# A hybrid decoder layer: the gate products of the recurrence as pairs of 64-row matmuls

## The chip, the cores and the metric

The kernel runs on one core of one Trainium2 chip. The time is the device time of one execution in microseconds (us), lower is better. A run's profile is one profiled execution. PE is TensorE, PEld its weight loads, DVE VectorE, ACT ScalarE, POOL GpSimd, and SP the engine that issues most DMAs.

## What is computed

One layer of a decoder over 16 meta tokens and 1024 tokens of width 1024, in float32. Behind a combined input projection stand sliding-window attention (8 heads of 64) and a gated linear recurrence of width 512 side by side; then an output projection, a normalization, and a feed-forward layer of width 4096. What the change touches is the recurrence's gates:

```python
def rg_lru(x, w_a, b_a, w_x, b_x, lam):
    xb = x.reshape(bsz, t, LRU_BLOCKS, LRU_BLOCK)          # 8 blocks of 64
    gate_r = jnp.einsum("btnc,ncd->btnd", xb, w_a).reshape(bsz, t, LRU_WIDTH) + b_a
    gate_i = jnp.einsum("btnc,ncd->btnd", xb, w_x).reshape(bsz, t, LRU_WIDTH) + b_x
    r, i = jax.nn.sigmoid(gate_r), jax.nn.sigmoid(gate_i)
    log_a = -LRU_C * r * jax.nn.softplus(-lam)
    a, mult = jnp.exp(log_a), jnp.sqrt(-jnp.expm1(2.0 * log_a))
    u = mult * (i * x)
    # h[t] = a[t] * h[t-1] + u[t]
```

Each of the 8 blocks has its own 64x64 matrix for either gate: the product is block diagonal.

## The kernel before

Every matrix product is done in three passes: an operand is split into a rounded high part and a low remainder (`split`, lines 94 to 101: ScalarE's copy is line 96, VectorE's subtraction line 99), and `mm3` (lines 123 to 129) adds high by high (L125), high by low (L126) and low by high (L127). Tiles come from tags with a fixed number of buffers each (`bufs`, line 55: 8 of tag c, 17 of b, 4 of d, 2 of e, and two PSUM banks each of s, pt, o and acc); a tile waits until a buffer of its tag is free. Each engine executes its instructions in a fixed order. A scheduler sets that order from the order of the program and its own model of the times, and `behind` (line 106) and `lut` (line 81, all activation functions with tables) add further constraints of order.

The work is laid out with channels on partitions and tokens along the free dimension. The stages:

- input rows are normalized and transposed, keys, values, the first queries and the first chunk of x are projected (to about 55 us);
- eight half steps of attention, between which the projections of the other queries, of x and of y are filled in (`next_fill`, line 694; eight of ten fills lie here);
- the recurrence, from about 200 to 270 us: `gates`, then the last two fills (y of chunks 2 and 3, `fill_y`, line 671), then `decay` and `recur` by pairs of chunks, GeLU of y, `rec_out`, and in between the loads and splits of the output weights;
- the output projection, residual and normalization by rows (from about 235 to 300 us, its first part beside the recurrence), and the feed-forward layer to the end.

The recurrence works on 4 chunks of 128 channels, two blocks of 64 each, over 1040 tokens. The biases and other per-channel parameters are loaded as rows of `prm_r` (lines 355 to 358) and transposed on PE into `prm` (line 470).

The gates' weights: `graw` holds for either gate and each chunk a block diagonal 128x128 matrix. GpSimd sets it to zero (line 718), four DMAs put the 64x64 blocks on the diagonals (line 722), and `split` makes the high and low halves `gh` and `gl` (line 727).

`gates(c)` (lines 731 to 749) splits the chunk's x into `ch` and `cl`, and for each gate and each of three pieces of 348, 348 and 344 tokens takes the next PSUM bank, runs `mm3` on full 128 rows, and has ScalarE apply the sigmoid with that gate's bias into a tile of tag c. Then VectorE multiplies the input gate by x (line 749). These are 24 pieces, 72 products and 24 sigmoids.

`decay(c)` computes Exp and Tanh of the recurrence gate, `recur(c)` the square root on ScalarE and then on VectorE lines 762 and 763 and the scan (line 764); `rec_out` multiplies by the gelu of y (line 769) and splits the result, which the output projection reads.

Of the kernel before, what the change touches and what calls it, by code (L numbers as in the profile page):

```python
# [10 lines left out]
F32R = mybir.dt.float32r  # L11
AF = mybir.ActivationFunctionType
ALU = mybir.AluOpType
# [3 lines left out]
P = 128  # L17
D = 1024
KC = D // P
T = 1024  # L20
NMETA = 16
TT = T + NMETA
HD = 64
NPAIR = 4
NLRU = 4
# [12 lines left out]
def hybrid_layer(  # L38
# [6 lines left out]
    nc = tc.nc  # L45
# [12 lines left out]
    def slot(tag, shape, dt=F32):  # L58
        uid[0] += 1
        return slab.tile(shape, dt, tag=tag, name=f"{tag}{uid[0]}", bufs=bufs[tag])  # L60
# [4 lines left out]
    def bank(tag, shape=(P, 512)):  # L65
        uid[0] += 1
        return ps.tile(list(shape), F32, tag=tag, name=f"ps_{tag}{uid[0]}")

    def f32(ap):
        return ap.bitcast(F32)  # L70
# [8 lines left out]
    last_lut = [None]  # L79

    def lut(*args, **kwargs):
        ins = nc.scalar.activation(*args, **kwargs).ins  # L82
        if last_lut[0] is not None:
            tc.add_manual_dep(
                ins, last_lut[0],
                mybir.DependencyInfo(
                    mybir.DependencyClass.NoSync, mybir.DependencyReason.DATA
                ),
                reason="lut",
            )  # L90
        last_lut[0] = ins.name
        return ins

    def split(hi, lo, src, eng=None):
        if eng is None:
            nc.scalar.copy(hi, src)  # L96
        else:
            eng.tensor_copy(hi, src)
        low = nc.vector.tensor_tensor(lo, src, f32(hi), op=ALU.subtract).ins  # L99
        mark[0] = low.name  # L100
        return low
# [4 lines left out]
    def behind(name, *inss):  # L106
        for ins in inss:
            tc.add_manual_dep(
                ins, name,
                mybir.DependencyInfo(  # L110
                    mybir.DependencyClass.NoSync, mybir.DependencyReason.DATA
                ),
                reason="order",
            )
# [8 lines left out]
    def mm3(dst, lhs, rhs, start, stop):  # L123
        (lh, ll), (rh, rl) = lhs, rhs
        nc.tensor.matmul(dst, lh, rh, start=start, stop=False, skip_group_check=True)  # L125
        nc.tensor.matmul(dst, lh, rl, start=False, stop=False, skip_group_check=True)  # L126
        last_mm[0] = nc.tensor.matmul(  # L127
            dst, ll, rh, start=False, stop=stop, skip_group_check=True
        ).ins.name
# [45 lines left out]
    last_pow = [None]  # L175
# [90 lines left out]
    HALF = (slice(0, HD), slice(HD, P))  # L266
# [9 lines left out]
    flip = [0]  # L276
# [77 lines left out]
    nc.sync.dma_start(nsink, attn_sinks[0].partition_broadcast(P))  # L354
    prm_r = slot("d", [8, 512])
    nc.sync.dma_start(prm_r[0:4, :], conv_w[0])
    for i, src in enumerate((conv_b, b_a, b_x, lru_lambda)):
        nc.sync.dma_start(prm_r[4 + i : 5 + i, :], src)


    vk = [slot("b", [P, 8, P], F32R) for _ in range(2)]
# [68 lines left out]
    for b in range(4):  # L430
# [3 lines left out]
        if b == 0:  # L434

            acc = [bank("acc"), bank("acc")]
# [11 lines left out]
            for w, (t0, n), sink in ((wq, (16, 256), sink_q0), (wx, piece, sink_x0)):  # L448
                acc = bank("acc")
# [10 lines left out]
    for h in range(2):  # L460
        r, o, m = HALF[h], HALF[1 - h], slice(P - NMETA, P)
# [72 lines left out]
    def at_pair(cp):  # L534
        for half in range(2):
            at[half][cp] = pair("b", [P, 2, 512])


    def scores(j, half, q):

        sn = slot("c", [P, 2, 4, P + 1])
        negm = small.tile([P, 2, 4], F32, name="negm", tag="negm")
        den = small.tile([P, 2, 4], F32, name="den", tag="den")
        rden = small.tile([P, 2, 4], F32, name="rden", tag="rden")
        for h in range(2):
            nc.gpsimd.tensor_copy(
                sn[:, h, :, P], nsink[:, j + 4 * h : j + 4 * h + 1].to_broadcast([P, 4])
            )
        for h in range(2):
            for bp in range(2):  # L550
                sp_ = bank("s", (P, 2, 256))

                def qk(dst, b, hi, lo):
                    c = slice(b * P, (b + 1) * P)
                    nc.tensor.matmul(
                        dst, q[h][:, c], hi, start=True, stop=False,
                        skip_group_check=True,
                    )
                    nc.tensor.matmul(
                        dst, q[h][:, c], lo, start=False, stop=True,  # L560
                        skip_group_check=True,
                    )

                for i in range(2):
                    b = 4 * half + 2 * bp + i
                    if b == 0:
                        qk(sp_[:, i, 0:P], b, km[:, h, :], km[:, 2 + h, :])
                        qk(sp_[:, i, P:256], b, khh[h][:, 0:P], kl[h][:, 0:P])
                    else:
                        c = slice((b - 1) * P, (b + 1) * P)  # L570
                        qk(sp_[:, i, :], b, khh[h][:, c], kl[h][:, c])
                s_ = sn[:, h, 2 * bp : 2 * bp + 2, 0:P]
                nc.scalar.copy(s_, sp_[:, :, P:256])
                nc.vector.copy_predicated(
                    s_, above_i.rearrange("p (a b) -> p a b", a=1).to_broadcast([P, 2, P]),
                    sp_[:, :, 0:P],
                )
                if half == 0 and bp == 0:
                    w = slice(0, P - NMETA)
                    nc.vector.copy_predicated(sn[:, h, 0, w], above_i[:, w], far)  # L580
            nc.vector.tensor_reduce(
                negm[:, h, :], sn[:, h], axis=mybir.AxisListType.X, op=ALU.min
            )
            for k in range(4):
                lut(
                    sn[:, h, k, :], sn[:, h, k, :], AF.Exp, scale=-1.0,
                    bias=negm[:, h, k : k + 1], accum_out=den[:, h, k : k + 1],
                )
            nc.vector.reciprocal(rden[:, h, :], den[:, h, :])
            nc.vector.tensor_tensor(  # L590
                sn[:, h, :, 0:P], sn[:, h, :, 0:P],
                rden[:, h, :].to_broadcast([P, 4, P]), op=ALU.mult,
            )
        return sn
# [45 lines left out]
    xc = [None] * NLRU  # L640
# [11 lines left out]
            )  # L652
        xc[c] = y

    ys = [None] * NLRU

    def fill_q(j):
        def run(w):
# [11 lines left out]

    def fill_y(c):
        def run(w):
            y = slot("b" if c == 1 else "d", [P, T])

            def sink(acc, t0, n):
                nc.vector.tensor_copy(y[:, t0 - NMETA : t0 - NMETA + n], acc)

            project(w, REAL2, sink)
            ys[c] = y
        return run  # L680
# [13 lines left out]
    def next_fill():  # L694
        i = len(loaded) - 1
        if i + 1 < len(fills):
            loaded.append(fills[i + 1][0]())
        else:
            loaded.append(None)
        fills[i][1](loaded[i])  # L700

    prev = None
    for j in range(NPAIR):
        for half in range(2):
            if j % 2 == 0 and half == 0:
                at_pair(j // 2)
            sn = scores(j, half, qs[j])
            if True:
                with deferred(FILL_LAG):
                    next_fill()  # L710
            if prev is not None:
                attend(*prev)
            prev = (j, half, sn)
    attend(*prev)


    graw = slot("e", [P, 2, NLRU, P])
    behind(last_pow[0], nc.gpsimd.memset(graw, 0.0).ins)
    for i, w in enumerate((w_a, w_x)):
        for s in range(2):  # L720
            r = slice(HD * s, HD * s + HD)
            nc.sync.dma_start(
                graw[r, i, :, r], w[0, s::2].rearrange("n c d -> c n d")
            )
    gh = slot("e", [P, 2, NLRU, P], F32R)
    gl = slot("b", [P, 2, NLRU, P], F32R)
    split(gh, gl, graw)

    rg = [None] * NLRU

    def gates(c):
        ch, cl = pair("b", [P, TT])
        split(ch, cl, xc[c])
        rg[c] = []
        for i in range(2):
            t_ = slot("c", [P, TT])
            for t0, n in ((0, 348), (348, 348), (696, 344)):
                flip[0] += 1
                acc = bank(("s", "pt", "o")[flip[0] % 3])
                mm3(  # L740
                    acc[:, :n], (gh[:, i, c, :], gl[:, i, c, :]),
                    (ch[:, t0 : t0 + n], cl[:, t0 : t0 + n]), True, True,
                )
                lut(
                    t_[:, t0 : t0 + n], acc[:, :n], AF.Sigmoid,
                    bias=prm[:, c, 5 + i : 6 + i],
                )
            rg[c].append(t_)
        nc.vector.tensor_tensor(t_, t_, xc[c], op=ALU.mult)

    av = [None] * NLRU

# [37 lines left out]

    for c in range(NLRU):
        gates(c)
    for _ in range(2):
        next_fill()
    for cs in ((0, 1), (2, 3)):
        for c in cs:
            decay(c)
# [606 lines left out]
```

## Time and profile before

| | us |
|---|---|
| three runs: median (lowest to highest) | 965.29 (964.68 to 965.95) |
| the profiled execution | 966.98 |
| its span, first to last instruction | 965.3 |
| mean granted clock of PE | 0.998 |

The page of the profile lists each engine's busy time, a chain of the work that ended last, followed back from the end, and groups of instructions by line. L82 is `lut`, so all of the sigmoids, exponentials and roots have that line; L96 and L99 are `split`, and L125 to L127 `mm3`, whichever stage calls them. So one goes by stretches of time and by the names of tiles: `ps_s<-b,e` with 348 columns is a gate product, `ps_acc<-a,ws` a projection. In a row of the timeline stand start, duration, engine, line, operation, output and inputs with their shapes, a count, and in brackets the idle time before it with what ended it.

### The profile page before, as it was taken

To read this page: it belongs to the slowest core of one execution; us is meant where nothing else is said; L and a number is where in the kernel's file an instruction comes from. 1 tells how busy PE (TensorE), PEld (TensorE's weight loads), DVE (VectorE), ACT (ScalarE), POOL (GpSimd) and SP (SyncE) were. 2 spreads that over 40 slices of the span, in tenths; PEclk is the share of its full clock that TensorE was granted. 3 is DMA by queue.
4 is the path that set the end of the run, shared out by engine and by line. 5 is a ranking of instruction groups with operands and counts; after the bars stand their busy time and mean duration, and the time that the engine had idled before them with its cause. 6 is when DMAs were issued, how large, how long until landed. Compare 5 with 4: busy or idle time off the path is not lost.

```text
span 965.3 us, 12356 instructions
## 1 busy us (share of the span) xinstructions
PE 947.6 (98%) x4718; PEld 795.0 (82%) x4718; DVE 651.6 (68%) x833; ACT 503.2 (52%) x845; POOL 120.5 (12%) x183
## 2 busy tenths in 40 slices
PE   6999999999999999999999999999999999999996
PEld 6999999888878877888888888888888888888885
DVE  5567988856865695665654455468557676779884
ACT  6546765567744663443555566654433343436441
POOL 4202544500011100000000000000111100001201
PEclk9999999999999999999999999999999999999999
DMA  8121010013235457576423264324687765547934
GB/s 278 37 56 40 24 44 23 25 49 81 88 129 156 157 173 237 180 254 201 173 87 106 92 202 130 103 91 122 163 186 183 193 210 206 184 144 195 240 66 88
DMA packets 88155, 130.14 MB, mean 135 GB/s; under 512 B 13688, under 2 KB 52616, under 8 KB 88096
## 3 DMA queue, kind: packets, MB, share of 16 engines
q1 hardware_dynamic: 79504, 106.54, 34.0%
q0 software_dynamic: 8160, 21.51, 10.8%
q10 hardware_dynamic: 432, 1.31, 0.4%
q8 instruction: 37, 0.61, 0.3%
q14 instruction: 22, 0.18, 0.1%
HBM read 109.93 MB, written 18.87 MB: 133 GB/s over the span
## 4 chain that ended last, share of the span: by engine, by line
PE 81%; DVE 8%; ACT 4%; issue 3%; DMA 3%; POOL 1%; SPq 0%; DVEq 0%; ACTq 0%; POOLq 0%
PE ps_acc L125 9%; PE ps_acc L127 9%; PE ps_acc L126 9%; PE ps_pt L125 6%; PE ps_pt L127 5%; PE ps_pt L126 5%; PE ps_s L127 5%; PE ps_s L125 5%; PE ps_s L126 5%; PE ps_o L125 5%; PE ps_o L126 5%; PE ps_o L127 5%; ACT c L82 1%; PE ps_acc L253 1%; PE ps_o L620 1%
## 5 line engine op out<-in xcount | busy, mean ns | idle before, releaser
L96 ACT CAST ws<-raw 128x1024 fp32r<-128x1024 f32 (+1 forms) x68 | 69.6, 1024 | 120.7 <-PE ps_o L126 50.5
L99 DVE TENSOR_TENSOR ws<-raw,ws 128x1024 fp32r<-128x1024 f32 (+1 forms) x69 | 82.3, 1193 | 46.0 <-ACT ws L96 45.9
L125 PE MATMUL ps_acc<-a,ws 128*128 128x256 f32 (+2 forms) x256 | 85.8, 335 | 0.1
L126 PE MATMUL ps_acc<-a,ws 128*128 128x256 f32 (+2 forms) x256 | 85.4, 334 | 0.0
L127 PE MATMUL ps_acc<-a,ws 128*128 128x256 f32 (+2 forms) x256 | 84.9, 332 | 0.0
L99 DVE TENSOR_TENSOR b<-b,b 128x1024 fp32r<-128x1024 f32 (+2 forms) x48 | 57.5, 1199 | 32.3 <-PE ps_o L126 19.4
L96 ACT CAST ws<-e 128x1024 fp32r<-128x1024 f32 x41 | 42.9, 1045 | 65.4 <-PE ps_o L126 45.9
L96 ACT CAST b<-b 128x1024 fp32r<-128x1024 f32 (+2 forms) x47 | 48.8, 1037 | 37.3 <-DVE b L905 37.3
L99 DVE TENSOR_TENSOR ws<-e,ws 128x1024 fp32r<-128x1024 f32 x41 | 50.1, 1222 | 19.6 <-ACT ws L96 19.6
L609 POOL TENSOR_SCALAR_AFFINE_SELECT c<-c 128x512 fp32r<-128x512 f32 x64 | 52.6, 837 | 71.8 <-ACT c L96 61.9
L125 PEld LDWEIGHTS ps_acc<-a,ws 128*128 128x128 f32 x256 | 48.2, 188 | 4.6 <-ACT c L396 0.4
L127 PEld LDWEIGHTS ps_acc<-a,ws 128*128 128x128 f32 x256 | 48.2, 188 | 4.3
L126 PEld LDWEIGHTS ps_acc<-a,ws 128*128 128x128 f32 x256 | 48.2, 188 | 4.0
L125 PE MATMUL ps_acc<-ws,b 128*128 128x512 f32 (+1 forms) x120 | 46.2, 386 | 0.0
L127 PE MATMUL ps_acc<-ws,b 128*128 128x512 f32 (+1 forms) x120 | 46.2, 385 | 0.0
L126 PE MATMUL ps_acc<-ws,b 128*128 128x512 f32 (+1 forms) x120 | 46.1, 384 | 0.0
L125 PE MATMUL ps_pt<-ws,b 128*128 128x512 f32 x112 | 44.3, 395 | 0.0
L126 PE MATMUL ps_pt<-ws,b 128*128 128x512 f32 x112 | 44.1, 394 | 0.0
L127 PE MATMUL ps_pt<-ws,b 128*128 128x512 f32 x112 | 44.0, 393 | 0.0
L125 PE MATMUL ps_s<-ws,b 128*128 128x512 f32 x110 | 43.5, 395 | 0.0
L127 PE MATMUL ps_s<-ws,b 128*128 128x512 f32 x110 | 43.4, 394 | 0.0
L126 PE MATMUL ps_s<-ws,b 128*128 128x512 f32 x110 | 43.3, 394 | 0.0
(394 smaller groups left out, 2658.9 us busy)
## 6 DMA issues: line engine op xcount, KB each, us to landing
raw<-in_w_ff_dram SPq DMA_DIRECT2D x61, 512.0 KB, 3.8
e<-in_w_ff_dram SPq DMA_DIRECT2D x45, 512.0 KB, 3.8
d<-in_w_ff_dram SPq DMA_DIRECT2D x12, 512.0 KB, 3.8
s_dram<-d POOLq DMA_DIRECT2D x12, 512.0 KB, 4.0
raw<-in_w_in_dram SPq DMA_DIRECT2D x9, 512.0 KB, 4.6
c<-in_x_dram SPq DMA_DIRECT2D x8, 512.0 KB, 9.1
d<-in_x_dram SPq DMA_DIRECT2D x8, 512.0 KB, 4.8
out_dram<-raw SPq DMA_DIRECT2D x8, 512.0 KB, 2.6
```

Source lines behind the costliest of these rows:

```text
L82: ins = nc.scalar.activation(*args, **kwargs).ins
L96: nc.scalar.copy(hi, src)
L99: low = nc.vector.tensor_tensor(lo, src, f32(hi), op=ALU.subtract).ins
L125: nc.tensor.matmul(dst, lh, rh, start=start, stop=False, skip_group_check=True)
L126: nc.tensor.matmul(dst, lh, rl, start=False, stop=False, skip_group_check=True)
L127: last_mm[0] = nc.tensor.matmul(dst, ll, rh, start=False, stop=stop, skip_group_check=True).ins.name
L253: last_mm[0] = nc.tensor.matmul(acc[:, :n], w[k // 2][:, kc, :], u[kc][k % 2][:, t0 : t0 + n], start=k == 0 and kc == 0, stop=k == last an ...
L609: nc.gpsimd.affine_select(out=p_[:, :, s], in_=f32(p_[:, :, 0]), pattern=[[0, 4], [g, P]], compare_op=op, fill=0.0, base=0, channel_multip ...
L620: nc.tensor.matmul(po[:, oc : oc + n], v, p_[:, pc : pc + n], start=first and k == 0, stop=last and k == 1, skip_group_check=True,)
```

## The change

The weights of either gate no longer form block diagonal matrices. `graw` becomes [128, 4, 128]: partitions 0 to 63 hold a chunk's first block and partitions 64 to 127 its second; along the columns stand the two gates of that block, the recurrence gate first in the first block, and the input gate first in the second. Nothing need be set to zero. High and low halves share a tile `gw`.

`gates(c)` now takes two PSUM banks for each piece of tokens. For each of the three passes it issues two products one after the other, on rows 0 to 63 and on rows 64 to 127, each with 128 columns of weights, and each into its own bank. Their results hold both gates of one block, so the sigmoid's outputs `z[0]` and `z[1]` hold both gates mixed. The biases are laid out to match (four DMAs in place of two).

A new function `gather(c)` puts them apart: VectorE copies the input gate of the first block and of the second into a tile `gi`, 64 partitions each, GpSimd copies the recurrence gate of the second block into `z[0]`, and VectorE multiplies `gi` by x. For chunks 0 and 1 it is called behind their gates; for chunks 2 and 3 behind the fill of y's chunk 2, and placed behind that fill's first copy on VectorE. y of chunk 2 and `gi` of chunks 2 and 3 take buffers of tag b. The rounding of the weights (`gw[:, 0]`) is placed behind the last table function that precedes the last half step of attention.

```diff
--- before.py
+++ after.py
@@ -354,8 +354,15 @@
     nc.sync.dma_start(nsink, attn_sinks[0].partition_broadcast(P))
     prm_r = slot("d", [8, 512])
     nc.sync.dma_start(prm_r[0:4, :], conv_w[0])
-    for i, src in enumerate((conv_b, b_a, b_x, lru_lambda)):
-        nc.sync.dma_start(prm_r[4 + i : 5 + i, :], src)
+    for i, src in ((4, conv_b), (7, lru_lambda)):
+        nc.sync.dma_start(prm_r[i : i + 1, :], src)
+
+    for i, src in enumerate((b_a, b_x)):
+        for s in range(2):
+            nc.sync.dma_start(
+                prm_r[5 + s : 6 + s, :].rearrange("o (c t k) -> t o c k", t=2, k=HD)[i ^ s],
+                src.rearrange("o (c t k) -> t o c k", t=2, k=HD)[s],
+            )
 
 
     vk = [slot("b", [P, 8, P], F32R) for _ in range(2)]
@@ -652,7 +659,7 @@
             )
         xc[c] = y
 
-    ys = [None] * NLRU
+    ys, y_copies = [None] * NLRU, {}
 
     def fill_q(j):
         def run(w):
@@ -670,10 +677,11 @@
 
     def fill_y(c):
         def run(w):
-            y = slot("b" if c == 1 else "d", [P, T])
+            y = slot("b" if c in (1, 2) else "d", [P, T])
 
             def sink(acc, t0, n):
-                nc.vector.tensor_copy(y[:, t0 - NMETA : t0 - NMETA + n], acc)
+                ins = nc.vector.tensor_copy(y[:, t0 - NMETA : t0 - NMETA + n], acc).ins
+                y_copies.setdefault(c, ins.name)
 
             project(w, REAL2, sink)
             ys[c] = y
@@ -704,6 +712,7 @@
         for half in range(2):
             if j % 2 == 0 and half == 0:
                 at_pair(j // 2)
+            gate_after = last_lut[0]
             sn = scores(j, half, qs[j])
             if True:
                 with deferred(FILL_LAG):
@@ -714,39 +723,53 @@
     attend(*prev)
 
 
-    graw = slot("e", [P, 2, NLRU, P])
-    behind(last_pow[0], nc.gpsimd.memset(graw, 0.0).ins)
+
+    graw = slot("e", [P, NLRU, P])
     for i, w in enumerate((w_a, w_x)):
         for s in range(2):
-            r = slice(HD * s, HD * s + HD)
             nc.sync.dma_start(
-                graw[r, i, :, r], w[0, s::2].rearrange("n c d -> c n d")
-            )
-    gh = slot("e", [P, 2, NLRU, P], F32R)
-    gl = slot("b", [P, 2, NLRU, P], F32R)
-    split(gh, gl, graw)
+                graw[HALF[s], :, HALF[i ^ s]],
+                w[0, s::2].rearrange("n c d -> c n d"),
+            )
+    gw = slot("e", [P, 2, NLRU, P], F32R)
+    behind(gate_after, nc.scalar.copy(gw[:, 0], graw).ins)
+    nc.vector.tensor_tensor(gw[:, 1], graw, f32(gw[:, 0]), op=ALU.subtract)
 
     rg = [None] * NLRU
 
     def gates(c):
         ch, cl = pair("b", [P, TT])
         split(ch, cl, xc[c])
-        rg[c] = []
-        for i in range(2):
-            t_ = slot("c", [P, TT])
-            for t0, n in ((0, 348), (348, 348), (696, 344)):
+
+
+        z = [slot("c", [P, TT]) for _ in range(2)]
+        for t0, n in ((0, 348), (348, 348), (696, 344)):
+            acc = []
+            for s in range(2):
                 flip[0] += 1
-                acc = bank(("s", "pt", "o")[flip[0] % 3])
-                mm3(
-                    acc[:, :n], (gh[:, i, c, :], gl[:, i, c, :]),
-                    (ch[:, t0 : t0 + n], cl[:, t0 : t0 + n]), True, True,
+                acc.append(bank(("s", "pt", "o")[flip[0] % 3]))
+            for k, (a, b) in enumerate(((0, ch), (0, cl), (1, ch))):
+                for s in range(2):
+                    nc.tensor.matmul(
+                        acc[s][:, :n], gw[HALF[s], a, c, :], b[HALF[s], t0 : t0 + n],
+                        start=k == 0, stop=k == 2, skip_group_check=True,
+                    )
+            for s in range(2):
+                lut(
+                    z[s][:, t0 : t0 + n], acc[s][:, :n], AF.Sigmoid,
+                    bias=prm[:, c, 5 + s : 6 + s],
                 )
-                lut(
-                    t_[:, t0 : t0 + n], acc[:, :n], AF.Sigmoid,
-                    bias=prm[:, c, 5 + i : 6 + i],
-                )
-            rg[c].append(t_)
-        nc.vector.tensor_tensor(t_, t_, xc[c], op=ALU.mult)
+        rg[c] = z
+
+
+    def gather(c):
+        z, gi = rg[c], slot("b" if c > 1 else "c", [P, TT])
+        first = nc.vector.tensor_copy(gi[HALF[0]], z[0][HALF[1]]).ins
+        nc.gpsimd.tensor_copy(z[0][HALF[1]], z[1][HALF[1]])
+        nc.vector.tensor_copy(gi[HALF[1]], z[1][HALF[0]])
+        nc.vector.tensor_tensor(gi, gi, xc[c], op=ALU.mult)
+        rg[c] = z[0], gi
+        return first
 
     av = [None] * NLRU
 
@@ -790,8 +813,12 @@
 
     for c in range(NLRU):
         gates(c)
-    for _ in range(2):
-        next_fill()
+        if c < 2:
+            gather(c)
+    next_fill()
+    for c in (2, 3):
+        behind(y_copies[2], gather(c))
+    next_fill()
     for cs in ((0, 1), (2, 3)):
         for c in cs:
             decay(c)
```

## The prediction, made before the change was run

> **What bounds the kernel now.** I read the page's busy line first, then the busy time by stretch around the gates, then the chain of waits there.
>
> ```profile
> PE 947.6 (98%) x4718; PEld 795.0 (82%) x4718; DVE 651.6 (68%) x833; ACT 503.2 (52%) x845; POOL 120.5 (12%) x183
> ```
> ```profile
> 203.50:221.20 17.70, 17.70 (x98) 16.27 (x98) 7.23 (x8) 13.84 (x27) 0.00 (x0) 1.00 0.12 31
> 221.20:229.50 8.30, 8.30 (x38) 6.77 (x37) 3.65 (x5) 8.19 (x8) 0.00 (x0) 1.00 0.25 62
> 229.50:269.36 39.86, 39.65 (x172) 31.82 (x171) 36.37 (x37) 27.02 (x33) 0.00 (x0) 1.00 0.28 88
> ```
> The columns are the stretch and its length in us, then busy time and count of PE, PEld, DVE, ACT and POOL, then the granted clock (1.00 throughout) and the DMA share. The gates lie in the first stretch. PE is busy all of it. VectorE works 7.23 of 17.70 us there, and 36.37 of 39.86 us in the third stretch, where the recurrence is computed. GpSimd does nothing in all three.
>
> The chain of waits runs, from the sigmoids on, not over PE but over ScalarE and VectorE:
>
> ```profile
> 218.71 0.96 ACT c L82 x2
> ...
> 221.17 1.28 ACT L82
> ...
> 228.39 1.08 ACT c L82
> 229.50 2.40 DVE c L762 x2
> ...
> 268.05 0.61 DVE d L769
> 268.69 0.63 ACT b L96
> 269.36 0.50 PE ps_pt L125
> ```
> Sigmoid, table load, Exp and Tanh, Sqrt, the recurrence, the product with the gelu, its rounding, and then the output projection on PE. PE has other work meanwhile (projections and output products of other chunks), and that work is used up just as the chain arrives:
>
> ```profile
> 269.36 0.50 PE L125 MATMUL ps_pt<-a,b 128*128 128x512 f32 x1 [0.21 <-ACT b L96]
> ```
> PE waits 0.21 us there. So between 201.6 and 269.36 there are **two bounds of almost one length**: PE's own work, and the chain that begins with the first sigmoid. The kernel gains the smaller of what the two gain. Behind 269.36 I see no stage held to a clock time of its own, so I let a gain there run through to the end.
>
> **PE's work.** Now there are 24 pieces of three products, 72 in all. First and last of one unbroken run of 21:
>
> ```profile
> 212.63 0.32 PE L125 MATMUL ps_s<-b,e 128*128 128x348 f32 x1
> ...
> 215.79 0.32 PE L127 MATMUL ps_s<-b,b 128*128 128x348 f32 x1
> ```
> 20 steps in 3.16 us are 0.158 us a step (the 0.32 us is one product's passage, half of it under the next). 72 x 0.158 = 11.4 us. Afterwards there are again 72 products, of the same columns but 64 rows each, in 36 pairs whose two members use different rows of the array and different PSUM banks. Call the step of a pair p. No row of this trace shows two products side by side, so p is bounded: below by 0.158, one product's step, if the members overlap wholly; above, as long as their weights still load ahead, by 0.316, two steps. For the weights I look at the only products on few rows that are followed by their like, the parameter transposes:
>
> ```profile
> 55.08 0.38 PE L306 MATMUL ps_o<-ident,d 128*128 128x128 f32 x2
> 55.29 0.38 PE L306 MATMUL ps_s<-ident,d 128*128 128x128 f32 x2
> 55.60 0.41 PE L469 MATMUL ps_o<-ident,d 8*128 8x8 f32 x4
> 55.95 0.44 PE L528 MATMUL ps_pt<-ident,c 128*128 128x128 f32 x2
> ```
> ```profile
> L469 PE MATMUL ps_o<-ident,d x4: 202/202/223, 55.6 to 55.8; 8*128 8x8 f32 x4
> ```
> Four of them, each with a weight load of 128 columns, take 0.41 us from first start to last end, and one takes 0.20 us, so they start 0.07 us apart. Two loads a pair, 0.14 us, fit under 0.158. I take p = 0.18, near the lower end, with 0.02 for the second member: 36 x 0.18 = 6.5 us, **4.9 us less**.
>
> By the Trainium skill (TensorE: Matmul & The Clock Gate, Part 3: packing small matmuls), products on different row groups start within about 4 ns of each other, and four row tiles gave 3.07 times the speed, 77% of four. At 77% of two, as an estimate from that page, p would be 0.206, and PE would save 4.0 us.
>
> What speaks against the change is in the same rows. The first 8-row load is not issued under the running transpose:
>
> ```profile
> 55.60 0.26 PEld L469 LDWEIGHTS ps_o<-ident,d 8*128 8x128 f32 x3 [0.17 <-issue]
> ```
> PEld stands 0.17 us idle although nothing is waited for. The full-row transposes step by 0.105 us (55.08 and 55.29 each head two); the next product begins about 0.2 us behind the last one, and on the way back 0.14 us behind. So **a change of rows costs about 0.1 us** (0.05 to 0.15). The Trainium skill (TensorEngine Tiling (Array Packing), Key Properties) has the rule: changing the tiling mode drains the array. The trace agrees, with this 0.17 us.
>
> How many changes? Between the gate products PE now runs projection products of full rows; their counts in five gaps:
>
> ```profile
> 202.52:202.98 0.46, 0.45 (x2) 1.00 0.00 0
> ...
> 204.91:208.13 3.22, 3.22 (x14) 1.00 0.00 0
> ...
> 210.53:210.75 0.22, 0.21 (x1) 1.00 0.00 0
> ...
> 211.24:212.62 1.38, 1.38 (x6) 1.00 0.00 0
> ...
> 215.95:218.02 2.07, 2.07 (x9) 1.00 0.79 202
> ```
> Five gaps make six stretches of gates, 12 changes, 1.2 us (0.6 to 1.8). PE in all: 36p + 1.2 - 11.4, which at p = 0.18 is **-3.7 us** (-5.1 to +1.8 from the bounds).
>
> **The chain's work.** Its first part is ScalarE's:
>
> ```profile
> 204.85 0.55 ACT L82 ACTIVATE c<-ps_s,prm 128x348 f32<-128x348 f32 x1
> ...
> 207.03 1.08 ACT L96 CAST b<-b 128x1040 fp32r<-128x1040 f32 x1
> ...
> 213.37 0.55 ACT L82 ACTIVATE c<-ps_s,prm 128x348 f32<-128x348 f32 x1 [1.38 <-PE ps_s L127]
> 213.81 0.55 ACT L82 ACTIVATE c<-ps_pt,prm 128x348 f32<-128x348 f32 x1
> ...
> 218.71 0.55 ACT L82 ACTIVATE c<-ps_pt,prm 128x348 f32<-128x348 f32 x1 [1.95 <-PE ps_pt L127]
> ...
> 220.60 0.55 ACT L82 ACTIVATE c<-ps_o,prm 128x344 f32<-128x344 f32 x1
> ```
> From 204.85 to 221.15 are 16.3 us. Sigmoids that wait for nothing step by 0.44 us: 24 x 0.44 = 10.6, and one rounding of 1.0 is between them, 11.6. The remaining 4.7 us are waits for PE (1.38 and 1.95 the longest). With the products ready 3.7 us or more sooner, up to **4.7 us** of this goes. ScalarE's count and shapes stay.
>
> Then VectorE, which gets 8 copies of 64x1040 (two a chunk), and GpSimd, which gets 4. The nearest rows:
>
> ```profile
> L98 DVE CAST ws<-raw x1: 694/694/694, 223.8 to 223.8; 128x1024 fp32r<-128x1024 f32 x1
> ```
> ```profile
> L644 DVE TENSOR_SCALAR d<-d,prm x2: 809/812/816, 102.8 to 140.7; 128x1040 f32<-128x1040 f32 x2
> ...
> L644 DVE TENSOR_SCALAR b<-d,prm x1: 1130/1130/1130, 178.6 to 178.6; 128x1040 f32<-128x1040 f32 x1
> ```
> ```profile
> 157.51 0.63 POOL L609 TENSOR_SCALAR_AFFINE_SELECT c<-c 128x512 fp32r<-128x512 f32 x1 [3.99 <-ACT c L96]
> ...
> 177.49 4.76 POOL L609 TENSOR_SCALAR_AFFINE_SELECT c<-c 128x512 fp32r<-128x512 f32 x4 [0.24 <-DVE c L99]
> ```
> A copy between SBUF tiles of 1024 columns took 0.69 us; the same tensor_scalar took 0.81 alone and 1.13 while GpSimd was at work beside it. I take 0.70 a copy, 5.6 us in all (up to 1.13, 9.0 us). GpSimd at 0.63 us for 512 columns alone and 1.2 beside VectorE needs 1.3 to 2.4 us a copy. Two places matter:
> - The gathers of chunks 0 and 1 fall in the first stretch, where VectorE has over 10 us free; the projections run on PE meanwhile. If that cover were gone, they would cost their 2.8 us.
> - The gathers of chunks 2 and 3 wait for y's copy and stand on VectorE's queue **ahead of the recurrence** (L762), with two copies and the product with x (now L749) each: 2 x (1.4 + 1.24) = 5.3 us. L762 could then start 4.7 us sooner, near 224.8, and between the last sigmoid (216.5) and there 8.3 us are free less two splits and copies of y (about 3 us now). They fit with nothing over; I charge 1.7 us of collision (0 to 4).
>
> ```profile
> L749 DVE TENSOR_TENSOR c<-c,d x3: 1234/1241/1242, 209.3 to 216.3; 128x1040 f32<-128x1040 f32 x3
> ```
> So the chain gains 4.7 - 1.7 = **3.0 us** (-0.5 to 5). Exp and Tanh of a chunk also wait for GpSimd's copy into z[0]: its 1.3 to 2.4 us lie under the later chunks' sigmoids for chunks 0 to 2, and chunk 3 is needed only at the second Exp round, 20 us later. The third chunk's tiles in tag c take the buffers that the first gathers free; that wait is in the 1.7.
>
> **Edits at nothing.** The memset goes from GpSimd, idle around it. The weights' split halves (VectorE's is 1.2 us before 198, under projections on PE); its rounding moves to behind the last softmax but one, long before use. Two DMA issues of biases are added on SP:
>
> ```profile
> 18.73 0.22 SPq L358 DMA_DIRECT2D d<-in_b_x_dram  x1
> 20.01 0.22 SPq L358 DMA_DIRECT2D d<-in_lru_lambda_dram  x1
> 21.34 2.21 SPq L198 DMA_DIRECT2D raw<-in_w_in_dram  x3
> ```
> They step by 1.3 us, so the weight load behind them starts up to 2.6 us later, and what they load is used first at 55.60; PE's work on other projections covers that. Without the cover it would be the 2.6 us.
>
> **The sum.** PE -3.7, chain -3.0; the smaller gain decides: -3.0 us. The profiled execution, 966.98 us with a span of 965.3, would become 964.0; against the median of the runs shown, 965.29, that is **962.3 us**.
>
> **Rivals.**
> - *The pairs do not run side by side* (the change doesn't do what it says). Then 36p grows: PE changes by 36p - 10.2. At p = 0.316 it is +1.2; and if each load waits for the product before it, as at the change of rows, about 0.25 us a product, p = 0.5 and +7.8. It turns slower by 0.2% from p = 0.34. For it: no overlap is seen in this trace, and the load at 55.60 did wait. Against: that wait shows at changes only; 8-row loads then follow each 0.07 us. Time 966.5 to 973, likeliest about 968.
> - *VectorE becomes the bound.* Sigmoids come sooner, but the late gathers (5.3 to 7.4 us) go into the third stretch, which has 3.5 us free; the chain ends where it ended or a little later, and PE stands idle instead. For it: 91% busy there. Against: 10 us free before. Time 964.5 to 966.5.
> - *Evacuation sets the pace.* By the Trainium skill (TensorEngine Tiling, PSUM Bottleneck), tiling speeds TensorE but not the emptying of PSUM. Here ScalarE's 11.6 us of the 16.3 are that limit, and the chain's 4.7 us already stop at it. If all else goes well, PE saves 5.1 and the chain 4.7: 960.6.
>
> **How the numbers follow.** Forecast, with its own range 960.6 to 963.3 us: 0.50. All goes well, 959.2 to 960.6: 0.12. VectorE the bound: 0.16. Pairs in sequence: 0.22, of which 0.02 near 966.5. A measurement of this kernel can tell 0.2%, 1.9 us, from no change. Faster 0.50 + 0.12 = 0.62; within 0.2%, 0.16 + 0.02 = 0.18; slower 0.20. The range leaves out the slowest sequences and the luckiest orders of instructions: 959.2 to 968.
>
> **What would show it.** In the profile after: pairs at L125's successor starting a few ns apart, with steps near 0.18 us; a gap of about 0.1 us at each change of rows; the sigmoids within 12 to 13 us; L762's first start near 226; PE's wait at the output projection's last chunk 0.5 to 1.5 us, filled by VectorE, not PE. Pair steps over 0.3 us, or L762 not earlier, would make it wrong, and so would a wait that grows behind 269 us.

## The result, and the profile after

| | before | after |
|---|---|---|
| median of six runs (lowest to highest), us | 965.71 (964.68 to 966.87) | 961.86 (960.82 to 963.93) |
| ratio, 95% interval | | 0.9962 (0.9951 to 0.9973) |
| profiled execution, its span, us | 966.98, 965.3 | 963.93, 962.1 |
| first gate product to first transpose behind the output projection, us | 201.59 to 291.21: 89.62 | 202.01 to 287.40: 85.39 |

The change took 3.85 us off; 962.3 us was forecast, 3.0 less than the 965.29 known then. The last row measures the stage by itself in the profiled executions, free of what varies ahead of it (in the thirteen profiles the first gate product lay between 199.96 and 202.99 us, whatever the kernel): 4.23 us less. It compares the same work: in it PE's timeline lists 335 products of 512 columns before and 336 after, besides the 72 of the gates. Later, between 340 and 380 us, where PE waits for the next stage's first operands, its waits grew from 1.43 to 1.79 us, so a little (0.36 us) is given back.

The busy line of the page after:

```profile
PE 943.7 (98%) x4718; PEld 789.4 (82%) x4718; DVE 658.9 (68%) x841; ACT 502.0 (52%) x845; POOL 125.0 (13%) x186
```
PE has the same 4718 products and 3.9 us less of busy time; VectorE has the eight copies and 7.3 us more. The gate products of the first chunk in PE's timeline after, from the last projection product ahead of them to the second behind:

```profile
201.69 0.40 PE L125 MATMUL ps_acc<-a,ws 128*128 128x512 f32 x1
202.01 0.43 PE L753 MATMUL ps_s<-b,e 64*128 64x348 f32 x1
202.02 0.42 PE L753 MATMUL ps_pt<-b,e 64*128 64x348 f32 x1
202.28 0.32 PE L753 MATMUL ps_s<-b,e 64*128 64x348 f32 x1
202.28 0.31 PE L753 MATMUL ps_o<-b,e 64*128 64x348 f32 x1
202.43 0.32 PE L753 MATMUL ps_pt<-b,e 64*128 64x344 f32 x1
202.44 0.32 PE L753 MATMUL ps_o<-b,e 64*128 64x344 f32 x1
...
203.38 0.32 PE L753 MATMUL ps_pt<-b,e 64*128 64x344 f32 x1
203.38 0.32 PE L753 MATMUL ps_o<-b,e 64*128 64x344 f32 x1
203.63 0.50 PE L126 MATMUL ps_acc<-a,ws 128*128 128x512 f32 x1
203.96 0.39 PE L127 MATMUL ps_acc<-a,ws 128*128 128x512 f32 x1
```
Two products start within 0.01 us of each other, and each is as long as a full-row one (0.32 us). From the second pair to the ninth the step is (203.38 - 202.28) / 7 = **0.157 us a pair**, where one full-row product took 0.158. The price stands at the ends: 0.32 us from the projection to the first pair (its own step is 0.23), 0.27 to the second, 0.25 from the last pair to the projection (a pair's step is 0.157), 0.33 to the next. Over the usual steps that is 0.09 + 0.11 us on the way in and 0.09 + 0.10 on the way out, so by these rows each change of rows costs about **0.2 us**. PEld's timeline shows the same hole at the change:

```profile
202.01 0.18 PEld L753 LDWEIGHTS ps_s<-b,e 64*128 64x128 f32 x1 [0.36 <-issue]
...
203.62 0.19 PEld L126 LDWEIGHTS ps_acc<-a,ws 128*128 128x128 f32 x1 [0.22 <-issue]
```
Each chunk's pairs stand in one stretch (starts 202.01, 207.30, 211.22 and 215.12), so there are 8 changes. ScalarE's sigmoids, first and last, and what it waited for:

```profile
204.44 0.55 ACT L82 ACTIVATE c<-ps_s,prm 128x348 f32<-128x348 f32 x1
...
208.13 0.55 ACT L82 ACTIVATE c<-ps_s,prm 128x348 f32<-128x348 f32 x1 [0.94 <-PE ps_pt L753]
...
212.06 0.55 ACT L82 ACTIVATE c<-ps_s,prm 128x348 f32<-128x348 f32 x1 [1.17 <-PE ps_pt L753]
...
215.96 0.55 ACT L82 ACTIVATE c<-ps_s,prm 128x348 f32<-128x348 f32 x1 [1.14 <-issue]
...
218.14 0.58 ACT L82 ACTIVATE c<-ps_o,prm 128x344 f32<-128x344 f32 x1
```
They take 14.3 us in place of 16.3. ScalarE still waits ahead of each chunk but the first (the profile names PE for two of the three waits), because PE's order puts projection products between the chunks' pairs. VectorE's timeline, the gather of chunk 2 and the start of the two recurrences:

```profile
215.75 0.70 DVE L767 COPY b<-c 64x1040 f32<-64x1040 f32 x1
216.49 0.69 DVE L769 COPY b<-c 64x1040 f32<-64x1040 f32 x1
217.21 1.98 DVE L770 TENSOR_TENSOR b<-b,d 128x1040 f32<-128x1040 f32 x1
...
227.14 2.39 DVE L785 SCALAR_TENSOR_TENSOR c<-b,c 128x1040 f32<-128x1040 f32 x2 [2.15 <-ACT c L82]
...
255.36 4.53 DVE L787 TENSOR_TENSOR_SCAN c<-b,b 128x1040 f32<-128x1040 f32 x2
```
The recurrence (L785) begins 2.36 us sooner by the clock of the trace, 2.8 us measured from the first gate product. It waited for ScalarE, not for the gathers ahead of it. The last two scans stand back to back from 255.36. Before, the last one began at 263.34:

```profile
256.50 2.31 DVE L764 TENSOR_TENSOR_SCAN c<-b,c 128x1040 f32<-128x1040 f32 x1
...
263.34 2.31 DVE L764 TENSOR_TENSOR_SCAN c<-b,c 128x1040 f32<-128x1040 f32 x1
```
In VectorE's timeline before, three splits of the output weights (253.06, 259.87 and 262.21, 1.2 us each) and a product with the gelu (261.00, two in 1.28) stand among the last two chunks' recurrences. After, all seven splits of these weights are done by 248.8, and the products stand behind the scans.

At the output projection PE waits for nothing any more:

```profile
262.00:266.80 4.80, 4.80 (x22) 3.91 (x21) 3.90 (x7) 1.74 (x4) 0.00 (x0) 1.00 0.31 109
266.80:290.00 23.20, 23.20 (x106) 18.96 (x106) 13.66 (x21) 11.60 (x31) 5.40 (x10) 1.00 0.26 98
```
So the chain that the prediction had as the nearer bound no longer holds PE up here. What follows tests this, and whether the overlap is really the source.

### The profile page after: what moved, and what is told of

Read it like the earlier page. It is cut to its first block, busy times and chain, and to the rows that moved or that the text cites. A ratio compares the mean times of both kernels' runs of the same rounds, so it can differ in the third digit from the quotient of the medians.

```text
span 962.1 us, 12377 instructions
## 1 busy us (share of the span) xinstructions
PE 943.7 (98%) x4718; PEld 789.4 (82%) x4718; DVE 658.9 (68%) x841; ACT 502.0 (52%) x845; POOL 125.0 (13%) x186
## 4 chain that ended last, share of the span: by engine, by line
PE 87%; DVE 5%; ACT 3%; DMA 2%; issue 1%; POOL 0%; SPq 0%; DVEq 0%; POOLq 0%; ACTq 0%
PE ps_acc L126 10%; PE ps_acc L125 10%; PE ps_acc L127 10%; PE ps_pt L127 6%; PE ps_pt L126 6%; PE ps_pt L125 6%; PE ps_s L127 6%; PE ps_s L126 6%; PE ps_s L125 6%; PE ps_o L127 5%; PE ps_o L126 5%; PE ps_o L125 5%; DMA raw<-in_w_ff_dram 1%; PE ps_acc L253 1%; ACT c L82 1%; PE ps_o L627 1%
```

## The experiments

Theory 1: the gain is the overlap of two products on different rows, PE sets the end of the stage, and the chain over ScalarE and VectorE has some slack after the change. Theory 2: sigmoids that come sooner make the gain, and the chain sets the end. Each kernel was timed beside the kernel before; a ratio is to that.

### No overlap: both products on the same rows

```diff
-                        acc[s][:, :n], gw[HALF[s], a, c, :], b[HALF[s], t0 : t0 + n],
+                        acc[s][:, :n], gw[HALF[0], a, c, :], b[HALF[0], t0 : t0 + n],
```


> After the change, but both products of a pair use rows 0 to 63 (the first block's gates are computed twice and the second block's not at all, so another result); order, counts, shapes, banks and changes of rows stay. Theory 1 (the gain is the overlap of two products on different rows): no overlap is left, 9 steps of 0.157 us more in each of four stretches, 5.7 us more than the pairs, ratio to before 1.002 (1.001 to 1.003); the trace shows 18 steps of 0.157 us a stretch. Rival (64-row products are quicker by themselves, or the gain is the sigmoids'): less than 3 us more, ratio under 0.9993.

Measured: 967.31 us, ratio 1.0007 (0.9998 to 1.0016), so 0.0045 or 4.3 us above the pairs, with the end of the interval near the 5.7. Its timeline of PE, the first stretch:

```profile
200.70 0.43 PE L753 MATMUL ps_s<-b,e 64*128 64x348 f32 x1
200.97 0.32 PE L753 MATMUL ps_pt<-b,e 64*128 64x348 f32 x1
201.13 0.32 PE L753 MATMUL ps_o<-b,e 64*128 64x348 f32 x1
...
203.50 0.32 PE L753 MATMUL ps_o<-b,e 64*128 64x344 f32 x1
```
Eighteen products start one after the other, 16 steps from 200.97 to 203.50 of 0.158 us. From first gate product to first transpose the stage takes 90.48 us, 5.1 more than with the pairs and 0.9 more than before, and PE waits for nothing in it. Everything else of the change is in this kernel: without the overlap it is worth nothing, if anything a little less.

### The blocks in turn

Of a chunk, all nine products of the first block, then all nine of the second. The chunk's six banks are taken first, and the sigmoids follow in the same order of blocks; shown is the order of the loops around the product:

```diff
-            for k, (a, b) in enumerate(((0, ch), (0, cl), (1, ch))):
-                for s in range(2):
+        for s in range(2):
+            for t0, n in pieces:
+                for k, (a, b) in enumerate(((0, ch), (0, cl), (1, ch))):
```


> The same 64-row products as after the change, but of a chunk all nine of the first block, then all nine of the second, so that neighbours in the order use the same rows of the array and only the one at the seam can overlap. Theory 1 (the gain is the overlap of two products on PE, and PE sets the end of this stage): 17 steps of 0.157 us a chunk in place of 9, +5.0 us on 961.9, so 966.9 us, ratio to before 1.0012. Theory 2 (the gain comes from sigmoids that start sooner, PE only follows): ScalarE's pace of 0.44 us a sigmoid still holds, and of the 5.0 us at most 1 to 3 show, 963 to 965 us, ratio 0.997 to 0.999.

Measured: 965.54 us, ratio 0.9983 (0.9974 to 0.9993). The time is inside theory 2's range. But in the first chunk the scheduler had mixed the blocks' products again, and in the others the two blocks overlap in a way that is shown below, so the run tells the theories apart badly; its stage takes 88.36 us, 3.0 more than with the pairs. In a second kernel each product of a chunk was put behind the one before it:

```diff
+                    if before:
+                        behind(before, ins)
+                    before = ins.name
```


> As the kernel with a chunk's blocks in turn, but with the order of the products of a chunk fixed one behind the other, so that no scheduler can put products on different rows side by side. Theory 1 (the gain is the overlap): 17 steps of 0.157 us a chunk in place of 9, 5.0 us more than the pairs, ratio to before 1.0014 (1.0004 to 1.0024). Theory 2 (earlier sigmoids make the gain): 1 to 3 us more than the pairs, ratio 0.997 to 0.999.

Measured: 966.95 us, ratio 0.9994 (0.9982 to 1.0005): 3.1 us above the pairs, between the two expectations. The trace says why it was not 5.0. In the order that the edit fixes, all of the first block's products (banks s, pt, o, three each) stand ahead of the second block's (s, pt, o again). The first rows of one chunk's stretch in PE's timeline:

```profile
208.24 0.74 PE L756 MATMUL ps_s<-b,e 64*128 64x348 f32 x3
208.83 0.64 PE L756 MATMUL ps_pt<-b,e 64*128 64x348 f32 x3
209.16 0.42 PE L756 MATMUL ps_s<-b,e 64*128 64x348 f32 x1
209.31 0.32 PE L756 MATMUL ps_o<-b,e 64*128 64x344 f32 x1
209.42 0.32 PE L756 MATMUL ps_s<-b,e 64*128 64x348 f32 x1
209.47 0.32 PE L756 MATMUL ps_o<-b,e 64*128 64x344 f32 x1
```
The second block's first product starts at 209.16, ahead of the first block's seventh at 209.31: the two halves of the rows run side by side for three products each, and their starts are out of program order. From its start to the next projection (210.78) this stretch takes 2.54 us. The pairs take 1.62 (202.01 to 203.63) and the pairs on the same rows 3.05 (200.70 to 203.75). So 4 x 0.92 = 3.7 us more were to be expected; the stage shows 89.26 - 85.39 = 3.9. (In the first chunk one product stands alone ahead of five projection products, which makes two changes of rows more.)

### The price of a change of rows

Twelve full-row products more (overwritten by the pairs that follow), once ahead of each piece, once three together ahead of each chunk:

```diff
+                nc.tensor.matmul(
+                    acc[0][:, :n], gw[:, 0, c, :], ch[:, t0 : t0 + n],
+                    start=True, stop=True, skip_group_check=True,
+                )
```


> After the change with one full-row product more ahead of each piece of gates (its result is overwritten), 12 in all, so that the pairs stand in 12 stretches in place of 4. Theory 1 (each stretch of pairs costs PE about 0.4 us of changes of rows, as the four stretches of the profile show it, and PE sets the end): 12 x 0.157 = 1.9 us of products and 8 x 0.4 = 3.2 us of changes, 967.0 us, ratio 1.0013. Rival (a change costs 0.05 to 0.1 us, the low end of the prediction): 1.9 + 16 x 0.05 to 0.1, 964.6 to 965.4 us, ratio 0.9988 to 0.9997. The chain sets the end: under 964.

> The control to the kernel with full-row products between the pieces: the same 12 products, but three ahead of each chunk's first piece, beside the projections that run there anyway, so no change of rows is added. Both theories of the change's price: 12 x 0.157 = 1.9 us, 963.8 us, ratio 0.998. If the chain has slack and sets nothing: the same. If the chain sets the end: 961.9 to 962.5 us.

Measured: between the pieces 968.63 us, ratio 1.0018 (1.0003 to 1.0032); ahead of the chunks 965.3 us, ratio 0.9989 (0.9978 to 1.0). The products alone cost 0.0027, 2.6 us where 1.9 were expected; PE also waited 0.4 us there for one of VectorE's copies. The 16 changes cost 0.0029, 2.8 us or 0.18 us each, against 3.2 expected and 2.4 at most by the prediction's price (0.05 to 0.15); the intervals leave 0.07 to 0.28 us a change, so the times alone do not rule that price out. PE's timeline of the first kernel shows the changes one by one:

```profile
206.04 0.32 PE L751 MATMUL ps_s<-b,e 128*128 128x348 f32 x1
206.29 0.42 PE L757 MATMUL ps_s<-b,e 64*128 64x348 f32 x1
206.30 0.43 PE L757 MATMUL ps_pt<-b,e 64*128 64x348 f32 x1
206.55 0.31 PE L757 MATMUL ps_s<-b,e 64*128 64x348 f32 x1
...
206.72 0.32 PE L757 MATMUL ps_pt<-b,e 64*128 64x348 f32 x1
206.97 0.42 PE L751 MATMUL ps_o<-b,e 128*128 128x348 f32 x1
```

Into the pairs, the steps are 0.25 us (206.04 to 206.29) and 0.26 (to 206.55), out of them 0.25 (206.72 to 206.97), where 0.157 is usual; the stretch behind began at 207.33, 0.36 us on. That is 0.39 us for one product put between, 3.1 us for eight. The stage shows only 2.0 us between the two kernels (89.99 against 87.99), 2.4 without the control's wait, which is 0.13 to 0.15 us a change. So the price is 0.13 to 0.2 us, and what makes the difference stays open. The times of the two kernels are a poor measure of it: in the profiled execution of the first (970.77 us, 2.1 above its median) PE also waits long behind the stage, 1.90 and 0.53 us near 460 us and 1.36 us near 755 us, which the control's does not.

### What the gather costs

VectorE multiplies z[1] by x, and the copies are left out:

```diff
-        first = nc.vector.tensor_copy(gi[HALF[0]], z[0][HALF[1]]).ins
-        nc.gpsimd.tensor_copy(z[0][HALF[1]], z[1][HALF[1]])
-        nc.vector.tensor_copy(gi[HALF[1]], z[1][HALF[0]])
-        nc.vector.tensor_tensor(gi, gi, xc[c], op=ALU.mult)
+        first = nc.vector.tensor_tensor(gi, z[1], xc[c], op=ALU.mult).ins
```


> After the change without the gather's copies on VectorE and GpSimd; VectorE multiplies z[1] by x at once, so the gates of the blocks stay mixed, and the result is another. Theory 1 (PE sets the end): nothing to be gained, 961.9 us, ratio 0.9960 within 0.0008. Theory 2 (the chain over ScalarE and VectorE sets the end, as the prediction's sum had it): the collision of the late gathers with the recurrence goes, 1.7 to 4 us less, 958 to 960 us, ratio 0.992 to 0.9943.

Measured: 963.28 us, ratio 0.9966 (0.9954 to 0.9978), as with the copies; the stage 85.07 us against 85.39. The gather is hidden, and theory 2's 1.7 us are outside the interval.

```diff
-        nc.gpsimd.tensor_copy(z[0][HALF[1]], z[1][HALF[1]])
+        nc.vector.tensor_copy(z[0][HALF[1]], z[1][HALF[1]])
```


> After the change with GpSimd's four copies given to VectorE. Theory 1 (PE sets the end; beside GpSimd's copy VectorE's product took 1.98 us where it took 1.24 before, as much as a third copy of 0.70 us): no change, ratio 0.9962 within 0.0012, VectorE's busy time the same within 0.5 us, its product back at 1.24 us. Rival (GpSimd relieves VectorE): 2.8 us more of VectorE, and up to 2 us more of time, ratio up to 0.998.

Measured: 962.71 us, ratio 0.9968 (0.9955 to 0.998). VectorE's timeline, chunk 2:

```profile
216.21 0.69 DVE L769 COPY b<-c 64x1040 f32<-64x1040 f32 x1
216.94 0.70 DVE L768 COPY c<-c 64x1040 f32<-64x1040 f32 x1
217.66 1.24 DVE L770 TENSOR_TENSOR b<-b,d 128x1040 f32<-128x1040 f32 x1
```
The product is back at 1.24 us, and VectorE's busy time is 659.1 us against 658.9. GpSimd's copy of chunk 2, in the kernel with it, overlaps the product of 217.21 that took 1.98 us:

```profile
216.58 1.51 POOL L768 COPY c<-c 64x1040 f32<-64x1040 f32 x1 [3.69 <-ACT c L82]
```
GpSimd's help saved VectorE nothing in all: beside its copies of 1.5 us, three of VectorE's four products took 0.74 us more each, as much as a copy.

### The chain's slack

The last chunk's scan is run twice (four times), on the kernel after and before:

```diff
-        nc.vector.tensor_tensor_scan(r, av[c], gi, 0.0, op0=ALU.mult, op1=ALU.add)
+        for _ in range(2 if c == 3 else 1):
+            nc.vector.tensor_tensor_scan(r, av[c], gi, 0.0, op0=ALU.mult, op1=ALU.add)
```


> After the change with the last chunk's scan run twice (the same result), 2.24 us more on the chain over VectorE just before its end. Theory 1 (PE sets the end, and the chain is done about 2 us before PE needs it): 0 to 0.4 us, ratio 0.9962 to 0.9967. Theory 2 (the chain sets the end): 2.2 us, ratio 0.9985.

Measured: 962.9 us, ratio 0.996 (0.9947 to 0.9972): no change that the interval can show, and theory 2's 0.9985 is outside it. The stage takes 86.61 us, 1.2 more than without the second scan.

> The kernel before with the last chunk's scan run twice, 2.24 us more on the chain. If the two bounds were of one length, as the prediction read it from PE's wait of 0.21 us: 2.0 to 2.2 us more, ratio 1.0021 to 1.0023. If the chain had slack in truth, because the order of VectorE's queue only put its end where PE needed it: 0 to 0.5 us, ratio 1.0000 to 1.0005.

Measured: 970.14 us, ratio 1.003 (1.0018 to 1.0041). PE's wait at the output projection, of the kernel after with one scan more, then of the kernel before with it:

```profile
265.89 0.50 PE L127 MATMUL ps_pt<-a,b 128*128 128x512 f32 x1 [1.00 <-DVE b L99]
```
```profile
273.12 0.50 PE L125 MATMUL ps_pt<-a,b 128*128 128x512 f32 x1 [2.57 <-ACT b L96]
```
Of 2.24 us more, 1.00 becomes a wait after the change, so the chain had 1.2 us to spare. Before it all becomes a wait (0.21 grew to 2.57): there the two bounds were of one length. But the stage grew by more than the chain, 3.9 us (93.55 against 89.62), and the time by 2.9 us (1.7 to 4.0).

> After the change with the last chunk's scan run four times, 6.7 us more on the chain. With one repetition PE waited 1.0 us of 2.24 for it, so the slack was about 1.2 us. Theory 1: 6.7 - 1.2 = 5.5 us more than the pairs, ratio to before 1.002. If the waits at PE's output products are paid back later by work that needs less waiting: 2 to 4 us, ratio 0.998 to 1.000.

Measured: 970.26 us, ratio 1.0038 (1.0025 to 1.0052): 7.3 us above the pairs, not 5.5. PE waits 4.57 us, and the stretches of 2 us behind its wait show what else it pays (after the five engines' busy times and counts stands the granted clock):

```profile
270.00:272.00 2.00, 1.06 (x4) 0.82 (x5) 1.92 (x4) 1.23 (x2) 0.00 (x0) 0.92 0.00 0
272.00:274.00 2.00, 2.00 (x6) 1.52 (x6) 0.22 (x1) 1.34 (x4) 0.00 (x0) 0.50 0.38 113
274.00:276.00 2.00, 2.00 (x8) 1.65 (x7) 1.18 (x3) 0.67 (x3) 0.56 (x1) 0.73 0.38 150
```
**Behind the wait the granted clock is 0.50 for some 3 us**, and the products step by 0.43 us in place of 0.23. Of the three stretches' 6 us, 0.16 + 1.0 + 0.54 = 1.7 us of clock are lost. With the wait that is 6.3 us, and the stage is 6.4 us longer than with the pairs (91.79 against 85.39). The kernel before with one scan more loses as much clock: 0.62 in 274 to 276 us and 0.53 in the next two, 1.7 us again. Its 3.9 us are 2.36 of wait and 1.7 of clock.

### Less work on PE before, and nothing else

```diff
-                mm3(
-                    acc[:, :n], (gh[:, i, c, :], gl[:, i, c, :]),
-                    (ch[:, t0 : t0 + n], cl[:, t0 : t0 + n]), True, True,
-                )
+                for k, a in enumerate((gh, gl)):
+                    nc.tensor.matmul(
+                        acc[:, :n], a[:, i, c, :], ch[:, t0 : t0 + n],
+                        start=k == 0, stop=k == 1, skip_group_check=True,
+                    )
```


> The kernel before with the gates' second pass (high weights by low input) left out, so another result: 24 products of 0.158 us less on PE, and nothing of the change besides. Theory 1 (what PE saves is what the kernel saves): 3.8 us less, ratio 0.9961. Two equal bounds, with sigmoids that come sooner by only a part of it: 1 to 3 us less, ratio 0.997 to 0.999.

Measured: 964.96 us, ratio 0.9979 (0.997 to 0.9988): 2.0 of 3.8 us. PE's waits in that kernel, and its clock behind them:

```profile
265.77 0.50 PE L125 MATMUL ps_pt<-a,b 128*128 128x512 f32 x1 [1.36 <-ACT b L96]
267.53 0.94 PE L127 MATMUL ps_pt<-a,b 128*128 128x512 f32 x2 [0.56 <-DVE b L99]
```
```profile
268.00:270.00 2.00, 2.00 (x7) 1.52 (x6) 0.08 (x1) 0.90 (x3) 0.00 (x0) 0.50 0.88 303
```
2.0 us of new waits (these two and one of 0.26, less the 0.21 of before) and 1.7 us of clock eat the 3.8 us: this stage does not gain (89.53 against 89.62). Where the 2.0 us of the times come from stays open: of the 2.9 us between the spans of the two profiled executions (965.3 and 962.4), 1.4 lie ahead of the stage, whose start varies by as much, and 1.4 behind it (0.8 of them waits between 338 and 379 us, 0.67 against 1.43). So with nearly as much taken from PE as the change took, the kernel before ran into its chain, and its stage gained nothing. With the change the stage gained 4.23 us, because the chain ended sooner as well. That the order of VectorE's work brought this is read from the timelines; no run changes that order alone.

## Why the prediction was right, step by step

The time came out near the forecast, 961.86 us for 962.3 and inside its own range, but in part by luck: the source of the gain was right, two pairs of errors cancelled, and the step that chose between the two gains failed.

- **PE's work** was right, by two sizes that were off against each other. A pair's step was put at 0.18 us and is 0.157: 36 x 0.157 = 5.7 us for 11.4, and 5.7 saved in place of 4.9. A change of rows was put at 0.1 us, read from transposes of 128 columns, and is about 0.2 by the rows; but there are 8 and not 12, 1.6 us in place of 1.2, because the three pieces of a chunk now fill all six banks at once and stand in one stretch. Together -4.1 us for a forecast -3.7; with the wait of 0.21 us that is gone, -4.3, and the stage shows -4.23.
- **The sigmoids** were to take 12 to 13 us and took 14.3. The waits for PE did not go: PE's order keeps projections between the chunks. The sigmoids gained 2.0 us of the forecast 4.7, and another 0.8 because the first one starts sooner behind the first gate product (2.43 us in place of 3.26).
- **The collision** of the late gathers with the recurrence, charged with 1.7 us, did not occur. The late gathers even took 6.9 us (215.75 to 222.66) where 5.3 were forecast, because a product beside GpSimd's copy takes 1.98 us and the sum has 1.24. (Of the two tensor_scalars read there as alone, one, at 102.78, ran beside GpSimd's work from 102.97.) Still L785 waited 2.15 us for ScalarE, and leaving the copies out gains nothing that can be measured. The two errors on the chain up to L785 cancel: 3.0 us were forecast, 2.8 came. (The range given for it, -0.5 to 5, is not worked out; its terms give 0.7 to 4.7.)
- **"The smaller gain decides: -3.0"** is the step that failed. PE's gain decided, not the chain's: -4.23 us in the stage. The reading of before was right (two bounds of one length: a scan more shows in full there), but I followed the chain only to L785 and took the rest of it as fixed. The rest is an order of VectorE's queue that the scheduler makes anew, and after the change the last scan starts at about 257.6 in place of 263.3, 6.2 us sooner measured from the first gate product, where L785 starts 2.8 sooner. PE's wait at the output projection, expected at 0.5 to 1.5 us, is gone, with 1.2 us to spare. That the chosen gain of 3.0 us lay so near the 3.85 measured is luck.
- **The rivals.** Pairs in sequence: the kernel with both products on the same rows is that case, and 1.0007 is its price. VectorE as the bound: it did not come, since PE waits for nothing in the stage; with 2.24 us more on VectorE's chain it waits 1.00 us, so it was near. Evacuation: the sigmoids took 14.3 us where ScalarE's own pace, 24 x 0.44, would be 10.6, so it did not set the pace. The edits at nothing cost nothing: the two bias DMAs more had the weight loads start at 22.93 in place of 21.34, and the first gate product came no later for it (199.96 to 202.01 us in the ten profiles with the change, 200.23 to 202.99 in the three without).
- By the Trainium skill (TensorE: Matmul & The Clock Gate, Part 3), four row tiles gave 3.07 times the speed, 77% of four. For two row tiles this trace has the full factor of two inside a stretch (0.157 us a pair against 2 x 0.158), so the estimate of 0.206 us a pair was too high here. The loss is at the ends of a stretch: with 9 x 0.157 + 0.4 = 1.8 us, a stretch is 1.57 times quicker than 18 x 0.158.

## What to carry to other kernels

Two matrix products that each use half of the rows cost one product's time (0.157 us against 0.158 here) when they stand side by side in the order, but each change between half and full rows costs 0.13 to 0.2 us, so keep their stretches long. When PE and a chain over other engines end together, work taken from one alone gains only until it waits for the other; look for what moves both. And a queue's order in a scheduled kernel is not fixed: a sum that follows a chain through it should say which part of that order it takes as given.

## What was not expected of the hardware

- A wait of PE can cost more than its length. Behind waits of 2.57 us and 4.57 us, and behind 1.36 us and 0.56 us close together, the granted clock fell to about a half, and 1.7 us were lost each time; behind one wait of 1.00 us it stayed at 1.00. The length does not decide alone. In the kernel with full-row products between the pieces, the clock stayed at 1.00 behind waits of 1.90 and 0.53 us, and what decides is not shown:

```profile
459.69 0.50 PE L125 MATMUL ps_s<-b,ws 128*128 128x512 f32 x1 [1.90 <-ACT ws L96]
460.94 0.50 PE L127 MATMUL ps_s<-b,ws 128*128 128x512 f32 x1 [0.53 <-DVE ws L99]
```
```profile
462.00:464.00 2.00, 2.00 (x10) 1.65 (x9) 1.90 (x4) 1.05 (x2) 0.29 (x1) 1.00 0.00 0
```
- Products on different rows of the array started out of program order: 209.16 ahead of 209.31 us above, in the kernel that fixes the order of a chunk's products. So the fixed order of PE is not the order of its starts.
- VectorE's product of two SBUF tiles took 1.98 us beside GpSimd's copy, 1.24 alone, while VectorE's copy that overlapped it (216.49) took 0.69 us, as without GpSimd's.
